# One transformer layer of a conformer on one core: another order of its head, of the LayerNorm sums and of one chunk, and other shares between engines

## The chip, the cores and the metric

The kernel runs on one core of one Trainium2 chip. The metric is the device time of one execution in microseconds. The median of three runs before the change is 1022.71 us (1021.47 to 1023.96).

The engines of the core are named as in the profile: PE is TensorE with its matmuls, PEld its weight loads, DVE is VectorE, ACT is ScalarE, POOL is GpSimd, and SP is SyncE, whose queue issues every DMA here.

## The reference, cut to what matters

With a depth of one, only the conformer layer on the 1024 latent tokens counts (the context is never read by it), followed by the MLP and a last norm. The width is 1024 and everything is float32.

```python
mod_l = (silu(c) @ w_mod + b_mod)                 # six vectors of 1024
sh1, s1, g1, sh2, s2, g2 = split(mod_l, 6)
h = rms_norm(x, norm1_g) * (1 + s1) + sh1
u = h @ w_pw1 + b_pw1                             # 1024 -> 2048
a, gate = split(u, 2)
u = a * sigmoid(gate)
u = dwconv(u, 31 taps, inside segments of 64 tokens) + b_dw
u = silu(layer_norm(u, ln_g, ln_b))
x = x + g1 * (u @ w_pw2 + b_pw2)
h = rms_norm(x, norm2_g) * (1 + s2) + sh2
x = x + g2 * (square(relu(h @ w1)) @ w2)          # 1024 -> 4096 -> 1024
return rms_norm(x, final_g)
```

## The kernel before

**Layout and blocks.** Tokens lie along the free axis and the 1024 channels in eight chunks of 128 partitions. The tokens are two blocks of 512, A (0) and B (1). Every product is done in three matmuls: a float32 operand is split into a rounded high part (a copy on ACT) and the remainder, the low part (a subtraction, L378, on DVE or POOL), and high x high, high x low and low x high are summed in a PSUM bank (L429 to L431, and L912 to L914 in the last product). One output unit of 128 channels for one block is eight times three matmuls of 128x512.

**The planner.** The program is written down as operations (class `Plan`, L86) with an engine, a modelled cost, buffers and a priority. `Plan.at` (L97) sets a base and every operation that follows gets the next rank above it. `Plan.run` (L125) simulates the engines: whenever one is free, it takes the ready operation of lowest rank whose tiles still find a place (`SLOTS`, `CAPS`, `KEEP`, L68 to L71). Operations that lie more than `NEAR` ranks past the oldest that is unplanned must leave some tiles free. The order so found is then emitted and is fixed: each engine takes its instructions in that order, whatever the real times are. A POOL operation planned after a DVE operation that is marked `port` is also made to wait for it (L231 to L235). The order of the DMAs on SP is found in the same way.

**The stages**, with their base ranks:

- *Head* (rank 0, L1045 to L1068). The eight chunks of x of block A are loaded, then the vector c, the identity and the small vectors. Squares on ACT and additions on DVE give one sum tile, which TensorE sums over partitions in turned form (four columns, L456). `rstd_of` (L498) takes the root on ACT, the reciprocal on DVE, spreads the four columns over a 128x512 tile (L519), and TensorE turns that into a row of factors in a bank (L528). Per chunk k, `mod_chunk` (L580) loads one 512 KB chunk of w_mod and reduces it against silu(c) (`csil`, L1054), for S1 and for SH1, on DVE (L587) or, elsewhere, on POOL with a second pass on ACT (L595, L600). `modulated` (L548) makes the split input, `first_weights` (L401) the split weights, and eight units of the first product are accumulated at once, k outermost. `warm` (L536) puts matmuls without use between, of 128 columns each.
- *Block B's input* (1010 to 1020), and then the rest of the first product: `PW1_ORDER` (1100 and up, L1100) lists pairs (block, chunk) of which each is two units (48 matmuls), a sigmoid on ACT and the gate on DVE (L640), through `first` (L1088).
- *Convolution* of block A (1200). Per chunk, 31 taps are shared out: on POOL (`POOL_TAPS`, ACT multiplies, POOL adds), on TensorE (`PE_TAPS`, a diagonal matrix per tap, L687, rank 1030), two or three as first taps on ACT, and the rest on DVE (L732). L742 and L751 join the partial sums.
- *LayerNorm* of block A (1300, `layer_norm`, L759): `cmean` holds the sum over channels of the convolution; TensorE sums what is left over partitions (`feed`, L448, L451). `direct` is how many chunks go to TensorE by themselves, while the others are added on another engine first. The mean is subtracted on DVE (L766), squares are summed the same way with `direct` = `LNA` or `LNB`, then root (L505), reciprocal (L507), multiplication (L780), silu and split.
- *Second convolution product* of block A (1400 and up, `pointwise2`), each output chunk with G1, S2 and SH2 through `mod_chunk`, on the engines of `G1_ENG`, `S2_ENG` and `SH2_ENG`. Then the second norm (1500), and the chunks of `PW1_LATE` (1600).
- *The MLP's first product* of block A, 32 units (2000 and up, `up_first`, L839), with block B's convolution, LayerNorm and second convolution product between them (`CONV_B`, `LN_B`, `PW2_B`).
- *The MLP's second product* (2200 and up, `mlp_joint`, L928), in eight groups that each combine two blocks and two halves into seven products instead of eight, each prepared by sums on DVE or POOL (`S_ENG`, `T_ENG`) and splits (`WLO_ENG`, `HLO_ENG`). The last group closes the final norms and stores the output.

Of the kernel before, what the change touches and what calls it, by code (L numbers as in the profile page):

```python
# [13 lines left out]
P = 128  # L14
D = 1024
# [23 lines left out]
POOL_TAPS = ((7, 8, 6, 9, 5, 5, 4, 3), (10, 9, 8, 7, 10, 6, 7, 5))  # L39

PW1_ORDER = (
    (0, 4), (0, 5), (1, 0), (1, 4), (1, 5),
    (0, 6), (0, 7), (1, 6), (1, 7), (1, 1),
)
PW1_LATE = ((1, 2), (1, 3))
# [3 lines left out]
PE_TAPS = ((2, 6, 2, 2, 2, 2, 5, 7), (0, 0, 2, 0, 0, 0, 0, 0))  # L49
PW2_LO, PW1_LO, WF_LO = "pool", "pool", ("dve",) * 8  # L50
UP_LO = ("dve", "pool")
S_ENG, T_ENG = ("pool", "pool", "dve", "dve"), ("dve", "dve", "dve", "dve")
GATE = 2
WLO_ENG, HLO_ENG = ("dve", "pool", "dve", "dve", "dve", "pool", "pool"), ("dve", "pool", "dve", "dve", "pool", "pool", "pool")
CM = (2, 1)
HEAD_DIRECT, LNA, LNB, N2B, FA = 0, 8, 2, 0, 0
TURNED = (True, False, False, False, False, False)
H1B_POOL = True
WARM = (8, 4, 6, 11)
# [3 lines left out]
S2_ENG, G1_ENG = ("pool", "pool", "dve", "pool", "pool", "pool", "pool", "pool"), ("pool", "pool", "pool", "dve", "dve", "pool", "dve", "pool")  # L63
SH2_ENG, G2_ENG = ("dve", "dve", "dve", "dve", "dve", "dve", "dve", "dve"), "dve"
# [5 lines left out]
NEAR = 120.0  # L70
CAPS = {"raw": 4, "head": 7, "w": 10, "tmp": 4, "tap": 3, "taps": 4, "acc": 8, "wave": 12}  # L71
# [10 lines left out]
class Op:  # L82
    __slots__ = ("eng", "costs", "emit", "prio", "turn", "table", "deps", "bufs", "left", "ready", "end", "after", "lag", "port")


class Plan:  # L86
# [38 lines left out]
    def run(self):  # L125
# [103 lines left out]
        for _, o in order:  # L229
            ins = o.emit()  # L230
# [15 lines left out]
def trunk(  # L246
# [50 lines left out]
    def c_dve(n):  # L297
        return 67 + 1.045 * n

    def c_stt(n):  # L300
        return 127 + 1.045 * n
# [138 lines left out]
    class Mean:  # L440
# [3 lines left out]
        def __init__(self, b, direct=1, eng="pool", turned=False):  # L444
            self.b, self.direct, self.eng, self.turned = b, direct, eng, turned
            self.n, self.sum, self.own, self.acc = 0, None, False, None

        def feed(self, x, first, last):  # L448
# [12 lines left out]
            if self.turned:  # L461
                plan.op("pe", 450 * QT, emit_turned, [x, ones], banks(self.acc))
            else:
                plan.op("pe", 1.67 * TB[self.b], emit, [x, ones], banks(self.acc))
# [33 lines left out]
    def rstd_of(mean, in_bank=True, hot=0):  # L498

        ((_, p),) = mean.acc  # L500
        if not mean.turned:
# [5 lines left out]
            plan.op("dve", 6.4 * TB[mean.b], lambda: dve.reciprocal(t(r), t(r)), [r], [r])  # L507
# [6 lines left out]
        warm(hot, root)  # L514
        plan.op("dve", 100, lambda: dve.reciprocal(root.t, root.t), [root], [root])
        spread = small(mean.b)
        plan.op(
# [8 lines left out]
        plan.op(  # L526
# [9 lines left out]
    def warm(n, after):  # L536
# [5 lines left out]
        def emit():  # L542
            for i in range(n):
                pe.matmul(t(p)[:, :P], ones.t, ones.t, start=True, stop=True)

        plan.op("pe", n * 220, emit, [ones, after], [p])
# [699 lines left out]
```

## Time and profile before

| | |
|---|---|
| median of 3 runs | 1022.71 us (1021.47 to 1023.96) |
| profiled execution, its own time | 1022.33 us |
| its span | 1020.5 us |
| PE busy | 980.4 us, 96% of the span, 4210 matmuls |
| DVE busy | 757.2 us, 74%, 1008 instructions |
| ACT busy | 520.1 us, 51%, 748 instructions |
| POOL busy | 513.8 us, 50%, 328 instructions |
| granted TensorE clock, mean | 0.981 |
| DMA | 125.28 MB, mean 123 GB/s |

A share of busy time is a mean over stages with different limits, so tables by stretch and timelines are read beside it. In a row of the timeline the first number is the start, the second the length, then engine, line, operation, tile written and tiles read, shapes and count; brackets give idle time of the engine before it and what ended it. A row that ends in a count merges neighbours of one line. A float32 matmul that isn't split, as in the sums (L451) and the taps (L687), appears as two instructions.

### The profile page before, as it was taken

The numbers are of one execution on the slowest core, as the hardware profiler recorded it, in microseconds if no ns is written. First come the engines' busy times: TensorE is split into PE (matmuls) and PEld (weight loads), VectorE is DVE, ScalarE is ACT, GpSimd is POOL, SyncE is SP. The second block draws the span as 40 slices with busy tenths as digits, with TensorE's granted clock in tenths as the row PEclk, the third lists the DMA queues.
The fourth block names the chain that finished last, engine by engine and source line by source line (L and its number), as shares of the span: only waits on it lengthen the run. The fifth ranks groups of instructions, "written<-read, shape, count | busy, mean of one in ns | idle before, by whom it ended". The sixth has DMA issues, their size and how long they took to land.

```text
span 1020.5 us, 11766 instructions
## 1 busy us (share of the span) xinstructions
PE 980.4 (96%) x4210; PEld 791.7 (78%) x4210; DVE 757.2 (74%) x1008; ACT 520.1 (51%) x748; POOL 513.8 (50%) x328
## 2 busy tenths in 40 slices
PE   5999999959999999999999999999999999999994
PEld 4878787638888888788888888888888888888882
DVE  5999999999699999863464473664747466494887
ACT  6488755185567765582473334342333434252443
POOL 0049999157744544322365536536363653634444
PEclk7999999979999999999999999999999999999998
DMA  9930025444426543644152413123141212303004
GB/s 358 404 114 1 1 83 208 163 164 165 145 83 215 182 158 116 224 157 155 67 192 87 141 41 104 62 83 124 62 144 42 99 66 83 125 1 124 1 1 165
DMA packets 52523, 125.28 MB, mean 123 GB/s; under 512 B 4464, under 2 KB 21104, under 8 KB 52464
## 3 DMA queue, kind: packets, MB, share of 16 engines
q1 hardware_dynamic: 52464, 124.53, 34.7%
q8 instruction: 33, 0.54, 0.2%
q14 instruction: 26, 0.21, 0.1%
HBM read 111.93 MB, written 12.58 MB: 122 GB/s over the span
## 4 chain that ended last, share of the span: by engine, by line
PE 75%; DVE 19%; POOL 2%; issue 2%; ACT 1%; DMA 1%; SPq 0%; POOLq 0%; DVEq 0%; ACTq 0%
PE bank L430 14%; PE bank L431 14%; PE bank L429 14%; DVE bank L732 12%; PE bank L913 10%; PE bank L914 10%; PE bank L912 10%; PE bank L451 2%; DVE big L378 1%; POOL small L378 1%; DVE bank L507 1%; DVE small L751 1%; POOL small L722 1%; DVE big L587 1%; DVE small L640 1%
## 5 line engine op out<-in xcount | busy, mean ns | idle before, releaser
L378 POOL TENSOR_TENSOR big<-big 128x1024 fp32r<-128x1024 f32 (+1 forms) x124 | 299.0, 2421 | 339.0 <-DVE big L378 155.6
L429 PE MATMUL bank<-big 128*128 128x512 f32 x896 | 355.0, 396 | 4.1 <-ACT big L371 3.9
L430 PE MATMUL bank<-big 128*128 128x512 f32 x896 | 350.0, 391 | 4.3 <-DVE big L378 3.2
L431 PE MATMUL bank<-big 128*128 128x512 f32 x896 | 349.7, 390 | 0.0
L800 DVE SCALAR_TENSOR_TENSOR small<-bank,mod,small 128x512 f32<-128x512 f32 x240 | 176.6, 748 | 197.1 <-PE bank L914 158.3
L378 DVE TENSOR_TENSOR big<-big 128x1024 fp32r<-128x1024 f32 (+2 forms) x160 | 198.6, 1262 | 27.4 <-POOL big L378 9.7
L872 ACT CAST big<-big 128x1024 fp32r<-128x1024 f32 x112 | 113.4, 1050 | 193.8 <-POOL big L378 60.0
L430 PEld LDWEIGHTS bank<-big 128*128 128x128 f32 x896 | 168.8, 188 | 42.8 <-DVE big L378 3.7
L732 DVE SCALAR_TENSOR_TENSOR bank<-small,vec,bank 128x464 f32<-128x464 f32 (+11 forms) x318 | 200.5, 697 | 1.7
L429 PEld LDWEIGHTS bank<-big 128*128 128x128 f32 x896 | 168.9, 188 | 41.8 <-ACT big L371 4.1
L431 PEld LDWEIGHTS bank<-big 128*128 128x128 f32 x896 | 168.8, 188 | 35.2
L912 PE MATMUL bank<-big 128*128 128x512 f32 x448 | 174.7, 390 | 0.0
L913 PE MATMUL bank<-big 128*128 128x512 f32 x448 | 174.3, 389 | 0.0
L914 PE MATMUL bank<-big 128*128 128x512 f32 x448 | 174.3, 389 | 0.0
L722 POOL TENSOR_TENSOR small<-small 128x400 f32<-128x400 f32 (+4 forms) x109 | 113.3, 1067 | 50.4 <-DVE big L378 27.8
L391 ACT CAST big<-big 128x1024 fp32r<-128x1024 f32 x92 | 95.6, 1043 | 23.4 <-POOL big L378 11.0
L912 PEld LDWEIGHTS bank<-big 128*128 128x128 f32 x448 | 84.1, 188 | 17.7 <-issue 0.2
L913 PEld LDWEIGHTS bank<-big 128*128 128x128 f32 x448 | 84.1, 188 | 17.6 <-issue 0.2
L914 PEld LDWEIGHTS bank<-big 128*128 128x128 f32 x448 | 84.1, 188 | 17.4
L378 POOL TENSOR_TENSOR small<-small 128x512 f32<-128x512 f32 x39 | 52.1, 1340 | 83.3 <-DVE big L378 44.3
L493 ACT ACTIVATE small<-small 128x512 f32<-128x512 f32 x64 | 39.0, 628 | 64.2 <-DVE small L800 60.0
L717 ACT ACTIVATE small<-small,vec 128x400 f32<-128x400 f32 (+4 forms) x109 | 62.9, 629 | 0.0
(68 smaller groups left out, 597.6 us busy)
## 6 DMA issues: line engine op xcount, KB each, us to landing
big<-in_w SPq DMA_DIRECT2D x96, 512.0 KB, 3.9
big<-in_wmod SPq DMA_DIRECT2D x48, 512.0 KB, 5.4
big<-in_wpw SPq DMA_DIRECT2D x28, 512.0 KB, 5.3
hidden<-small SPq DMA_DIRECT2D x32, 256.0 KB, 2.4
big<-hidden SPq DMA_DIRECT2D x16, 512.0 KB, 3.9
small<-in_xA SPq DMA_DIRECT2D x16, 256.0 KB, 5.2
big<-in_wfirst SPq DMA_DIRECT2D x8, 512.0 KB, 10.2
small<-in_xB SPq DMA_DIRECT2D x16, 256.0 KB, 6.1
```

What stands on the lines that cost most here:

```text
L378: lambda: eng_of[o.eng].tensor_tensor(out=out(), in0=a(), in1=b(), op=op), r, w, part=part, port=port,
L391: plan.op("act", c_act(D), lambda: act.copy(t(wh), t(raw)), [raw], [wh], also=[wl])
L429: pe.matmul(o, wh, hi(a)[:, s], start=first, stop=False)
L430: pe.matmul(o, wh, lo(a)[:, s], start=False, stop=False)
L431: pe.matmul(o, wl, hi(a)[:, s], start=False, stop=last)
L722: return pool.tensor_tensor(out=dst, in0=dst, in1=seg(t(m))[:, :, tt], op=ALU.add)
L732: dve.scalar_tensor_tensor(out=dst, in0=src, scalar=w, in1=dst, op0=ALU.mult, op1=ALU.add)
L800: lambda s=s, p=p: dve.scalar_tensor_tensor(out=t(x)[:, s], in0=cut(s, p), scalar=scale.t, in1=t(x)[:, s], op0=ALU.mult, op1=ALU.add,),
L872: plan.op("act", c_act(D), lambda: act.copy(t(h), t(x)), [x], [h], also=[l])
L912: pe.matmul(t(p), t(wh)[:, cs], t(hh)[:, ns], start=first and k == 0, stop=False, skip_group_check=not first)
L913: pe.matmul(t(p), t(wh)[:, cs], t(hl)[:, ns], start=False, stop=False, skip_group_check=not first)
L914: pe.matmul(t(p), t(wl)[:, cs], t(hh)[:, ns], start=False, stop=k == 1, skip_group_check=not first)
```

## The change

**Head.** The load of c and its silu move ahead of x and of the squares, so that the roots' table is loaded only once on ACT. The reductions of S1 (all but the first) and of SH1 are held until the spread tile (L519) is written (`hold`). `first_weights` moves behind `modulated`. The warm-up matmuls have other counts and are placed behind the fifth square, the turned sum and the spread product; a warm-up is now tied to an operation and no longer to a buffer.

**LayerNorm.** The sums of block A's mean and of its squares on TensorE (`feed`) get rank 1030, ahead of the first products (1100 and up). `rstd_of` places warm-ups behind the last sum and behind the reciprocal of block A's LayerNorm. `CM` gives block A's mean one direct chunk instead of two, and `LNB` block B's squares none instead of two.

**Order.** Chunk (1,2) moves from `PW1_LATE` to the end of `PW1_ORDER`; from the eleventh entry on, the loads of weights wait for the gate of the entry three places earlier (`PW1_BACK`). (0,6) and (0,7) come ahead of (1,4) and (1,5). Block B's taps on TensorE get rank 1399 instead of 1030.

**Shares.** Taps on POOL: block A 47 to 45, block B 62 to 56. Taps on TensorE: A 28 to 25, B 2 to 8. Reductions of G1, S2 and SH2 on DVE: 3, 1 and 8 before, 0, 2 and 1 after; the others are on POOL. Some sums and splits of the last product change engines.

**Planner.** `NEAR` is 250 instead of 120, one more tile for POOL's taps is allowed, and DVE's operations are modelled as 8 ns and 23 ns longer.

```diff
-POOL_TAPS = ((7, 8, 6, 9, 5, 5, 4, 3), (10, 9, 8, 7, 10, 6, 7, 5))
+POOL_TAPS = ((7, 7, 6, 9, 4, 5, 4, 3), (10, 9, 8, 4, 5, 7, 8, 5))
...
-    (0, 4), (0, 5), (1, 0), (1, 4), (1, 5),
-    (0, 6), (0, 7), (1, 6), (1, 7), (1, 1),
+    (0, 4), (0, 5), (1, 0), (0, 6), (0, 7),
+    (1, 4), (1, 5), (1, 6), (1, 7), (1, 1), (1, 2),
...
-PW1_LATE = ((1, 2), (1, 3))
+PW1_LATE = ((1, 3),)
+TAP_PRIO = (1030, 1399)
+PW1_BACK = 3
...
-PE_TAPS = ((2, 6, 2, 2, 2, 2, 5, 7), (0, 0, 2, 0, 0, 0, 0, 0))
+PE_TAPS = ((2, 6, 2, 3, 2, 2, 2, 6), (0, 0, 2, 3, 3, 0, 0, 0))
...
-S_ENG, T_ENG = ("pool", "pool", "dve", "dve"), ("dve", "dve", "dve", "dve")
+S_ENG, T_ENG = ("pool", "dve", "dve", "dve"), ("dve", "pool", "dve", "dve")
...
-WLO_ENG, HLO_ENG = ("dve", "pool", "dve", "dve", "dve", "pool", "pool"), ("dve", "pool", "dve", "dve", "pool", "pool", "pool")
-CM = (2, 1)
-HEAD_DIRECT, LNA, LNB, N2B, FA = 0, 8, 2, 0, 0
+WLO_ENG, HLO_ENG = ("dve", "pool", "pool", "dve", "dve", "dve", "dve"), ("dve", "pool", "pool", "dve", "pool", "dve", "pool")
+CM = (1, 1)
+HEAD_DIRECT, LNA, LNB, N2B, FA = 0, 8, 0, 0, 0
...
-WARM = (8, 4, 6, 11)
+WARM = (6, 6, 7, 11)
...
-S2_ENG, G1_ENG = ("pool", "pool", "dve", "pool", "pool", "pool", "pool", "pool"), ("pool", "pool", "pool", "dve", "dve", "pool", "dve", "pool")
-SH2_ENG, G2_ENG = ("dve", "dve", "dve", "dve", "dve", "dve", "dve", "dve"), "dve"
+S2_ENG, G1_ENG = ("pool", "pool", "dve", "pool", "pool", "pool", "dve", "pool"), ("pool", "pool", "pool", "pool", "pool", "pool", "pool", "pool")
+SH2_ENG, G2_ENG = ("pool", "pool", "pool", "pool", "pool", "pool", "dve", "pool"), "dve"
...
-NEAR = 120.0
-CAPS = {"raw": 4, "head": 7, "w": 10, "tmp": 4, "tap": 3, "taps": 4, "acc": 8, "wave": 12}
+NEAR = 250.0
+CAPS = {"raw": 4, "head": 7, "w": 10, "tmp": 4, "tap": 4, "taps": 4, "acc": 8, "wave": 12}
...
-        return 67 + 1.045 * n
+        return 75 + 1.045 * n
...
-        return 127 + 1.045 * n
+        return 150 + 1.045 * n
...
-                plan.op("pe", 1.67 * TB[self.b], emit, [x, ones], banks(self.acc))
+                o = self.fed = plan.op("pe", 1.67 * TB[self.b], emit, [x, ones], banks(self.acc))
+                if self.prio:
+                    o.prio = self.prio
...
-            plan.op("dve", 6.4 * TB[mean.b], lambda: dve.reciprocal(t(r), t(r)), [r], [r])
+            warm(hot, p.writers[-1] if p is not r else mean.fed)
+            o = plan.op("dve", 6.4 * TB[mean.b], lambda: dve.reciprocal(t(r), t(r)), [r], [r])
+            warm(hot, o)
...
-        warm(hot, root)
...
-    cmean = [Mean(0, CM[0]), Mean(1, CM[1])]
+    cmean = [Mean(0, CM[0], prio=1030), Mean(1, CM[1])]
...
-                plan.op("pe", 1.67 * reach(s, k), emit, [diag, u], [p]).prio = 1030
+                plan.op("pe", 1.67 * reach(s, k), emit, [diag, u], [p]).prio = TAP_PRIO[b]
...
-        ms = Mean(b, direct, turned=TURNED[1 + 2 * b])
+        ms = Mean(b, direct, turned=TURNED[1 + 2 * b], prio=1030 if b == 0 else None)
...
-        rstd = rstd_of(ms)
-        if b == 0:
-            warm(WARM[3], rstd)
+        rstd = rstd_of(ms, True, WARM[3] if b == 0 else 0)
...
-    xs0 = load_x(0)
     craw = new("big", [P, D], F32, "raw")
     plan.op("dma", 1460, lambda: sp.dma_start(t(craw), cvec.partition_broadcast(P)), w=[craw], lag=2000)
+    xs0 = load_x(0)
     load(ident, eye, P)
     load(vec, vecs, NVEC)
+    plan.op("act", c_act(D), lambda: act.activation(csil.t, t(craw), AF.Silu), [craw], [csil], "silu")
     ms = Mean(0, HEAD_DIRECT, "dve", TURNED[0])
-    warm(WARM[0], xs0[3])
     for k in range(KC):
         sq = add_square(ms, xs0[k])
-    plan.op("act", c_act(D), lambda: act.activation(csil.t, t(craw), AF.Silu), [craw], [csil], "silu")
+        if k == 4:
+            warm(WARM[0], sq.writers[-1])
     preload(AF.Sqrt, "sqrt", sq)
-    r0, r0_bank = rstd_of(ms, False, WARM[1])
-    warm(WARM[2], r0)
+    warm(WARM[1], ms.fed)
+    r0, r0_bank = rstd_of(ms, False)
+    warm(WARM[2], ms.spread_fed)
...
-        mod_chunk(S1, k, cap="head")
-        mod_chunk(SH1, k, "dve", "head")
-        wf.append(first_weights(k, WF_LO[k]))
+        mod_chunk(S1, k, cap="head", hold=[ms.spread] if k else ())
+        mod_chunk(SH1, k, "dve", "head", hold=[ms.spread])
         scale_column(sc1[k], mod[S1][k], C_N1, k)
         h1[0].append(modulated(0, xs0[k], r0 if k else r0_bank, sc1[k], mod[SH1][k], True))
+        wf.append(first_weights(k, WF_LO[k]))
...
-                w_of[c, h] = weights(wpw1[2 * c + h], PW1_LO, (), h1[0][KC - 1 :])
+                w_of[c, h] = weights(wpw1[2 * c + h], PW1_LO, after, h1[0][KC - 1 :])
...
-        first(*bc)
+        first(*bc, [us[PW1_ORDER[n - PW1_BACK]]] if n >= 10 else ())
```

More of the change, by code (lines that the diff above doesn't have):

```diff
@@ L82 @@
 class Op:
-    __slots__ = ("eng", "costs", "emit", "prio", "turn", "table", "deps", "bufs", "left", "ready", "end", "after", "lag", "port")
+    __slots__ = ("eng", "costs", "emit", "prio", "turn", "table", "deps", "bufs", "left", "ready", "end", "after", "lag", "port", "ins")
 class Plan:
@@ L229, in run @@
         for _, o in order:
-            ins = o.emit()
+            ins = o.ins = o.emit()
             if o.eng == "dve" and o.port:
@@ L440, in trunk, with __init__ @@
     class Mean:
-        def __init__(self, b, direct=1, eng="pool", turned=False):
+        def __init__(self, b, direct=1, eng="pool", turned=False, prio=None):
+            self.prio = prio
             self.b, self.direct, self.eng, self.turned = b, direct, eng, turned
@@ L461, in feed @@
             if self.turned:
-                plan.op("pe", 450 * QT, emit_turned, [x, ones], banks(self.acc))
+                self.fed = plan.op("pe", 450 * QT, emit_turned, [x, ones], banks(self.acc))
             else:
-                plan.op("pe", 1.67 * TB[self.b], emit, [x, ones], banks(self.acc))
+                o = self.fed = plan.op("pe", 1.67 * TB[self.b], emit, [x, ones], banks(self.acc))
+                if self.prio:
+                    o.prio = self.prio
         def add(self, x):
@@ L513, in rstd_of @@
         )
-        warm(hot, root)
         plan.op("dve", 100, lambda: dve.reciprocal(root.t, root.t), [root], [root])
         spread = small(mean.b)
-        plan.op(
+        mean.spread = plan.op(
             "dve", c_stt(TB[mean.b]),
@@ L525, in rstd_of @@
         )
-        plan.op(
+        mean.spread_fed = plan.op(
             "pe", 1.67 * TB[mean.b],
@@ L543, in emit @@
             for i in range(n):
-                pe.matmul(t(p)[:, :P], ones.t, ones.t, start=True, stop=True)
-        plan.op("pe", n * 220, emit, [ones, after], [p])
+                ins = pe.matmul(t(p)[:, :P], ones.t, ones.t, start=True, stop=True)
+                if i == 0 and after.eng != "pe":
+                    behind(ins, after.ins)
+        plan.op("pe", n * 213, emit, [ones], [p], gate=[after])
     def modulated(b, x, rstd, scale, shift, in_place, eng="dve"):
@@ L578, in modulated, with mod_chunk @@
         return out
-    def mod_chunk(v, i, eng="dve", cap="raw", gate=()):
+    def mod_chunk(v, i, eng="dve", cap="raw", gate=(), hold=()):
         raw = new("big", [P, D], F32, cap)
@@ L589, in mod_chunk @@
                 ),
-                [raw, csil, vec], [raw, m], port=True,
+                [raw, csil, vec], [raw, m], port=True, gate=hold,
             )
@@ L1086, in trunk, with first @@
     w_of = {}
-    def first(b, c):
+    def first(b, c, after=()):
         out = []
```

## The prediction, made before the changed kernel was run

> **What bounds the kernel now.** I read the page's head first, then busy time by stretch, then the timeline of the one long stretch in which TensorE has nothing to do. First the span and a table of stretches (start:end, length, then busy us and instructions of PE, PEld, DVE, ACT, POOL, then the granted clock, DMA share, GB/s).
>
> ```profile
> span 1020.5 us, 11766 instructions
> 10.00:23.60 13.60, 8.39 (x32) 6.60 (x32) 9.17 (x17) 10.39 (x17) 0.00 (x0) 0.57 1.03 406
> 23.60:66.00 42.40, 42.40 (x187) 35.12 (x188) 40.98 (x70) 22.00 (x35) 2.01 (x1) 1.00 0.85 330
> 150.00:199.80 49.80, 49.69 (x203) 37.49 (x202) 48.74 (x80) 21.74 (x43) 30.04 (x23) 1.00 0.53 185
> 199.80:228.20 28.40, 14.96 (x45) 7.40 (x44) 27.48 (x47) 19.82 (x32) 14.98 (x8) 0.79 0.46 157
> 228.20:290.00 61.80, 61.77 (x258) 50.25 (x259) 49.32 (x73) 37.58 (x60) 43.13 (x31) 0.96 0.44 154
> 350.00:410.00 60.00, 60.00 (x267) 49.67 (x266) 59.50 (x91) 39.04 (x61) 26.89 (x25) 1.00 0.39 136
> 540.00:1002.90 462.90, 462.90 (x2041) 382.88 (x2040) 289.30 (x328) 178.59 (x212) 232.33 (x99) 1.00 0.22 77
> 1002.90:1020.50 17.60, 3.68 (x8) 1.06 (x7) 11.89 (x14) 3.68 (x6) 7.46 (x6) 0.74 0.64 238
> ```
>
> TensorE is full before and after the hole from 199.8 to 228.2, and there it sets the pace: 462.9 us over 2041 matmuls is 0.227 us each, so an output unit of 24 matmuls takes 5.44 us, and one chunk of the first product for one block (two units) 10.9 us. What can be won lies in the head (23.6 us), in the hole, in TensorE work that goes away, and in the tail (17.6 us), whose order the change hardly touches. The profiled execution took 1022.33 us, 1.83 more than its span; I sum against it, and the median of the runs shown, 1022.71, is 0.4 above. About 0.2% (2 us) is what a measurement can tell from no change.
>
> The hole in the timeline (start, length, engine, line; the last three rows are from the chain that ended last):
>
> ```profile
> 196.66 0.69 DVE L751 TENSOR_TENSOR small<-bank,small 128x512 f32<-128x512 f32 x1
> 199.62 2.74 PE L451 MATMUL bank<-small,ones 128*128 128x512 f32 x6
> 207.12 4.87 DVE L766 TENSOR_TENSOR small<-small,bank 128x512 f32<-128x512 f32 x8
> 208.66 9.15 PE L451 MATMUL bank<-small,ones 128*128 128x512 f32 x16 [6.30 <-ACT small L493]
> 217.65 2.62 PE L544 MATMUL bank<-ones 128*128 128x128 f32 x22
> 218.55 3.37 DVE L507 RECIPROCAL bank<-bank 128x512 f32<-128x512 f32 x1 [0.85 <-ACT bank L505]
> 221.95 4.87 DVE L780 TENSOR_TENSOR small<-small,bank 128x512 f32<-128x512 f32 x8
> 228.23 0.79 PE L430 MATMUL bank<-big 128*128 128x512 f32 x1 [3.24 <-DVE big L378]
> 229.45 0.43 PE bank L429
> 234.03 0.23 PE bank L429
> 501.16 0.86 PE bank L451 x2
> ```
>
> Block A's convolution ends with L751 at 197.4. Its mean is summed on TensorE (three 512-wide sums of two instructions) by 202.4, but VectorE subtracts it only from 207.1, because other work stands ahead in its written order. Squares, eight sums, root, reciprocal, multiply, silu and split follow; dense products return at 228.2, at half pace (0.43 us) until about 233. The old row of products simply ran out.
>
> **The change part by part.** *The hole.* Chunk (1,2) of the first product, 10.9 us of TensorE, moves from behind block A's second norm to the end of that row. Its cost stays; it now lies where TensorE was idle. The LayerNorm sums (1030) rank above products (1100 and up), so they wait for at most the group of three in flight (0.68 us). Ten sums remain (mean 3 to 2, squares 8), at 0.86 us each at full clock (the last row above): 8.6 us.
>
> When is the chain done? Three rows: VectorE's taps, its modulation reductions, and TensorE's taps alone in a stretch of the table.
>
> ```profile
> L732 DVE SCALAR_TENSOR_TENSOR bank<-small,vec,bank 128x456 f32<-128x456 f32 (+10 forms) x158 | 101.6, 698 | 1.7
> L587 DVE CUSTOM_DVE_ANT_0 big<-big,csil,vec x36: 1273/1280/3490, 14.7 to 348.4; 128x1024 f32<-128x1024 f32 x36
> 150.00:199.80 49.80, 9.78 (x24) 4.20 (x24) 1.00 0.53 185
> ```
>
> A VectorE tap is 101.6/158 = 0.64 us. Block A has 157 of them now and 162 after (POOL 47 to 45, TensorE 28 to 25), +3.2; one reduction of 1.28 that stands among them goes to POOL: the convolution ends at 199.3. Mean by 201.0, eight subtractions (4.9) to 205.9, last square and sum to 208, root 0.7, reciprocal 3.4, multiplies from 212.1; products were dense 6.3 us after the multiplies began (228.2 less 221.95), so at 218.4. TensorE's own side: a tap there is two instructions, 9.78/12 = 0.82 us; three fewer end the old row at 196.9 instead of 199.4, and 10.9 and 8.6 more end at 216.4. On paper 2 us stay idle. The order is fixed ahead, and VectorE came 4.7 us late to its subtraction; I add half of that and take 4 us, with 0 and 12 as ends. The old stretch cost 28.4 us and another 2.3 at half pace (12 matmuls in 5.06 us instead of 2.7). The new one has 8.6 + 4 of it: **-18.1**.
>
> [...]
>
> *TensorE work.* Its taps go from 30 to 33 (A 28 to 25, B 2 to 8): +3 x 0.82 = **+2.5**. Block B's rank below the first products and need chunks that come late, so they lie in full stretches. Block B's LayerNorm sums go from three to one: **-1.7**; two more additions on POOL lie under 24-matmul units. Warm-up matmuls stay in idle time; if that is gone, 22 of them cost 2.6 us (the L544 row).
>
> *The head.*
>
> ```profile
> 12.13 1.87 PE L456 MATMUL bank<-ones,small 128*128 128x1 f32 x8 [7.37 <-DVE small L378]
> 10.76 1.28 ACT L1031 ACT_TABLE_LOAD   x1
> 12.37 1.28 ACT L1054 ACT_TABLE_LOAD   x1
> 13.66 1.06 ACT L1054 ACTIVATE csil<-big 128x1024 f32<-128x1024 f32 x1
> 14.73 1.28 ACT L512 ACT_TABLE_LOAD   x1
> 17.16 0.17 DVE L515 RECIPROCAL root<-root 128x4 f32<-128x4 f32 x1
> 20.91 0.75 DVE L553 SCALAR_TENSOR_TENSOR small<-small,sc,bank 128x512 f32<-128x512 f32 x1 [1.52 <-ACT small L533]
> ```
>
> Sums are done at 14.0, but the root starts only behind the last of three table loads, at 16.0, and its reciprocal at 17.2, behind two reductions. With cvec's load and silu first, one root load is left, before the sums end; holding the reductions for the spread removes the second wait. That is 17.16 - 14.4 = 2.8 us. Against it: cvec's 512 KB ahead of x delay the squares by up to 1.3 us at 406 GB/s; and VectorE, 40.98 of 42.4 us busy from 23.6 to 66, must deliver just as much sooner. I take **-2.2**, ends 0 and -3.
>
> *Shares and what comes later.* Nine more reductions move from VectorE to POOL (G1, S2, SH2), and each needs a pass on ACT (1.06 us for this width).
>
> ```profile
> L595 POOL TENSOR_TENSOR big<-big,csil x12: 2342/2378/2427, 99.4 to 266.7; 128x1024 f32<-128x1024 f32 x12
> L378 POOL TENSOR_TENSOR big<-big 128x1024 fp32r<-128x1024 f32 x2 | 4.7, 2350 | 25.1 <-DVE mod L587 18.1 <-ACT big L391 6.9
> 258.75 2.67 DVE L587 CUSTOM_DVE_ANT_0 big<-big,csil,vec 128x1024 f32<-128x1024 f32 x1
> L800 DVE SCALAR_TENSOR_TENSOR small<-bank,mod,small 128x512 f32<-128x512 f32 x8 | 6.0, 750 | 11.0 <-PE bank L431 11.0
> 409.75 1.41 DVE L751 TENSOR_TENSOR small<-bank,small 128x512 f32<-128x512 f32 x2
> 464.54 0.75 DVE L800 SCALAR_TENSOR_TENSOR small<-bank,mod,small 128x512 f32<-128x512 f32 x1 [4.24 <-PE bank L431]
> 497.18 0.75 DVE L800 SCALAR_TENSOR_TENSOR small<-bank,mod,small 128x512 f32<-128x512 f32 x1 [3.56 <-PE bank L431]
> 509.29 2.07 DVE L572 SCALAR_TENSOR_TENSOR big<-small,mod,big 128x512 fp32r<-128x512 f32 x3
> 500.57 0.60 ACT L843 ACTIVATE small<-bank 128x512 f32<-128x512 f32 x1 [1.03 <-POOL small L378]
> 517.94 0.59 ACT L843 ACTIVATE small<-bank 128x512 f32<-128x512 f32 x1
> ```
>
> POOL gets 9 x 2.38 = 21.4 us. From 150 to 228.2 it has 19.8 + 13.4 = 33.2 idle, much of it behind VectorE's reductions (18.1 in one wait). ACT has 28 + 8.6 idle there for about 10. So I cost it at nothing for TensorE; if the cover is gone, block A's weight splits on POOL come late (second rival). VectorE gains 11.5 us, and chunk (1,2) gives it taps in the 11.0 us in which it waited for TensorE, against 2 more taps of block B (1.3).
>
> TensorE reaches the time around 450 some 20 us ahead of before. Block B's convolution, which ends at 411 and then holds up block B's second product (464), must gain nearly as much. It gets 2.2 from the head, 9.8 from the earlier restart, 11.5 and part of 11.0: 23 or more. Besides, four units of the up product (21.8 us; ACT's L843 rows from 500 to 518) are still there to bridge block B's norm. So no new hole is priced. From 540 on each engine but TensorE has over a third of its time free (289 of 463 for VectorE); one 1.2 us operation more on VectorE per group, one of 2.4 fewer on POOL, and the planner's farther look ahead (250) cost nothing, ends -1 and +4.
>
> **Sum**: 1022.33 - 18.1 + 2.5 - 1.7 - 2.2 = 1002.8, say **1003**, 1.9% faster.
>
> **The rivals.**
> 1. *A wait takes the place of the hole.* TensorE's order is fixed. A sum ranked ahead of products and ready later than planned stops chunk (1,2) behind it. For: VectorE's 4.7 us delay. Against: the cost of a tap is raised to what the rows show. Price: idle 12 instead of 4, and 1.3 for the head: 1012.
> 2. *Slower: POOL's queue holds the split of (1,2)'s weights.* These splits are on POOL, behind nine more multiplications, and POOL waits for VectorE by order. If the 25.1 us of such waits in the L378 POOL row stay and fall ahead of the split, TensorE stands there, and the LayerNorm sums behind it. 1003 + 25.1 = 1028; it decides from 20 us of delay. Against: reductions on VectorE, which caused 18.1 of it, go, and the weights are gated two chunks ahead (some 22 us).
> 3. *Port.* The L587 at 258.75 took 2.67 instead of 1.28 beside a POOL operation. If each of nine POOL multiplications stops VectorE for its 2.38, block B's convolution loses 21.4 of its 23, and the bridge of 21.8 less about 13 for block B's norm (last L800 of its second product, 497.9, to its first three splits, 511) leaves 9: hole 20 - 2 - 9 = 9 us, 1012. [...]
> 4. *Nothing*: the hole only moves to block B's norm, 1022: VectorE's convolution would have to gain nothing.
>
> **How the numbers follow.** Forecast 0.60 (own range 998 to 1009), first rival 0.14, third 0.10, nothing 0.05, slower 0.11. Faster 0.84, same 0.05, slower 0.11. Leaving out the slower case and small remainders, the range goes from 995 (1003 less 0.8 for the head, 4 for a full hole and 1 later is 997, and 2 for a measurement) to 1019, between the 1012 of two rivals and the 1022 and 1028 left out in part.
>
> **What would show it.** Right: chunk (1,2)'s matmuls between 195 and 220, L766 within 1 us of the mean sum, a full clock there, dense products of block A's second convolution product near 216, one table load between the squares and the first root, products from about 21.4, no gap from 220 to 1000. Wrong: TensorE waiting over 5 us for ACT squares or a POOL split near 200; POOL full from 200 to 290; a TensorE gap between 400 and 520; VectorE's reductions in the head delaying the eighth input chunk.

## The result, and the profile after

| | before | after |
|---|---|---|
| median | 1022.49 us (1021.47 to 1023.96, 4 runs) | 1010.25 us (1009.33 to 1010.97, 4 runs) |
| ratio, 95% interval | | 0.9883 [0.9869, 0.9897] |
| profiled execution, its own time | 1022.33 us | 1009.33 us |
| first dense products | 23.58 us | 22.22 us |
| block A's convolution ends | 197.35 us | 199.93 us |
| dense products behind the LayerNorm | 228.2 us | 222.88 us |
| last product ends | 1002.88 us | 988.60 us |

The change makes the kernel 12.2 us faster. The forecast was 1003 (995 to 1019): the direction and the range held, and a third of the gain is missing. The medians are compared with runs of before on the same chip, the traces with the profiled execution of before. All the single edits below are planned anew by the planner, so the orders differ in more than the edit; the waits of each trace, more than its time alone, carry the conclusions. Three executions of two of these edits, of 1110, 1719 and 2580 us, lie far from the others of their kernels and are left out of the figures.

The head of the page of after, busy time by engine (span 1007.5 us):

```profile
PE 977.7 (97%) x4234; PEld 791.7 (79%) x4234; DVE 770.4 (76%) x1005; ACT 525.3 (52%) x767; POOL 510.6 (51%) x324
```

Busy time by stretch of after (columns as in the prediction's table), cut at the same events as there:

```profile
150.00:198.95 48.95, 48.95 (x203) 37.74 (x201) 47.11 (x77) 30.01 (x57) 48.57 (x33) 1.00 0.65 239
198.95:222.90 23.95, 21.39 (x100) 15.30 (x100) 23.88 (x41) 22.08 (x35) 15.48 (x9) 1.00 0.45 150
222.90:290.00 67.10, 66.10 (x282) 52.72 (x283) 65.57 (x92) 48.05 (x80) 49.52 (x35) 1.00 0.43 149
...
410.00:540.00 130.00, 129.85 (x569) 106.51 (x568) 71.48 (x73) 71.94 (x96) 45.27 (x30) 1.00 0.41 144
540.00:988.60 448.60, 448.55 (x1975) 370.12 (x1973) 302.39 (x330) 173.99 (x207) 210.10 (x90) 1.00 0.23 76
988.60:1007.50 18.90, 3.70 (x9) 1.44 (x8) 10.60 (x12) 2.71 (x5) 7.96 (x7) 0.72 0.59 222
```

The LayerNorm's stretch now has 21.4 of 24 us busy at a granted clock of 1.00, against 15 of 28.4 at 0.79; warm-ups, which do no useful work, are 4.8 of the 21.4 and 2.6 of the 15. From there to the last product TensorE lacks about 1 us before 290 and nearly nothing later. The tail got longer: 18.9 us against 17.6.

TensorE (L454 sums, L550 warm-ups, L431 and L432 products), DVE and ACT in the timeline of that stretch of after:

```profile
199.25 0.68 DVE L759 TENSOR_TENSOR small<-bank,small 128x512 f32<-128x512 f32 x1
199.98 1.12 PE L454 MATMUL bank<-small,ones 128*128 128x512 f32 x2 [1.03 <-DVE small L759]
201.25 4.86 DVE L774 TENSOR_TENSOR small<-small,bank 128x512 f32<-128x512 f32 x8
203.02 2.74 PE L454 MATMUL bank<-small,ones 128*128 128x512 f32 x6
206.29 4.45 PE L454 MATMUL bank<-small,ones 128*128 128x512 f32 x10
207.75 0.63 ACT L498 ACTIVATE small<-small 128x512 f32<-128x512 f32 x1
210.56 1.28 ACT L510 ACT_TABLE_LOAD   x1
212.56 3.36 DVE L513 RECIPROCAL bank<-bank 128x512 f32<-128x512 f32 x1
215.46 1.28 ACT L639 ACT_TABLE_LOAD   x1
215.95 3.08 DVE L786 TENSOR_TENSOR small<-small,bank 128x512 f32<-128x512 f32 x5
216.04 5.07 PE L550 MATMUL bank<-ones 128*128 128x128 f32 x44
217.46 1.28 ACT L791 ACT_TABLE_LOAD   x1
220.87 0.48 PE L431 MATMUL bank<-big 128*128 128x512 f32 x1
222.88 0.50 PE L432 MATMUL bank<-big 128*128 128x512 f32 x1 [1.53 <-DVE big L380]
```

The mean's subtraction (L774) starts 0.15 us behind the mean's sum; the old 4.7 us of delay are gone. Useful TensorE work ends at 216.04. From there warm-ups fill 4.8 us and another 2.0 pass around a single product, until the low part of the first split (L380) is there. With the 1.03 us ahead of the mean's sum that is 7.9 us without useful work.

### The profile page after: what moved, and what is told of

It is laid out like the page before. It is cut to its first block, busy times and chain, and to the rows that moved or that the text cites. A ratio compares the mean times of both kernels' runs of the same rounds, so it can differ in the third digit from the quotient of the medians.

```text
span 1007.5 us, 11799 instructions
## 1 busy us (share of the span) xinstructions
PE 977.7 (97%) x4234; PEld 791.7 (79%) x4234; DVE 770.4 (76%) x1005; ACT 525.3 (52%) x767; POOL 510.6 (51%) x324
## 4 chain that ended last, share of the span: by engine, by line
PE 82%; DVE 11%; issue 2%; ACT 2%; POOL 1%; DMA 1%; SPq 0%; POOLq 0%; DVEq 0%
PE bank L432 17%; PE bank L431 17%; PE bank L433 17%; PE bank L919 9%; PE bank L920 9%; PE bank L918 9%; DVE bank L740 2%; DVE big L380 2%; PE bank L695 2%; DVE big L595 2%; POOL small L380 1%; DVE small L380 1%; DVE bank L513 1%; DVE small L774 1%; DMA small<-in_xA 1%
## 5 line engine op out<-in xcount | busy, mean ns | idle before, releaser
L380 POOL TENSOR_TENSOR big<-big 128x1024 fp32r<-128x1024 f32 (+1 forms) x116 | 278.0, 2410 | 332.5 <-DVE big L380 108.7
L431 PE MATMUL bank<-big 128*128 128x512 f32 x896 | 355.9, 397 | 0.9 <-ACT small L639 0.9
L432 PE MATMUL bank<-big 128*128 128x512 f32 x896 | 348.9, 389 | 1.8 <-DVE big L380 1.5
L806 DVE SCALAR_TENSOR_TENSOR small<-bank,mod,small 128x512 f32<-128x512 f32 x240 | 177.6, 748 | 156.2 <-PE bank L920 126.5
L380 DVE TENSOR_TENSOR big<-big 128x1024 fp32r<-128x1024 f32 (+2 forms) x168 | 218.3, 1327 | 36.6 <-ACT big L878 9.3
L740 DVE SCALAR_TENSOR_TENSOR bank<-small,vec,bank 128x424 f32<-128x424 f32 (+10 forms) x325 | 202.8, 695 | 2.2 <-ACT bank L677 1.0
L432 PEld LDWEIGHTS bank<-big 128*128 128x128 f32 x896 | 168.2, 188 | 40.4 <-issue 3.7
L431 PEld LDWEIGHTS bank<-big 128*128 128x128 f32 x896 | 168.2, 188 | 39.4 <-issue 3.8
L730 POOL TENSOR_TENSOR small<-small 128x392 f32<-128x392 f32 (+4 forms) x101 | 106.1, 1075 | 39.2 <-ACT small L725 15.5
L380 POOL TENSOR_TENSOR small<-small 128x512 f32<-128x512 f32 x42 | 56.8, 1357 | 92.4 <-DVE big L380 48.4
L918 PEld LDWEIGHTS bank<-big 128*128 128x128 f32 x448 | 84.1, 188 | 17.7 <-issue 0.2
L725 ACT ACTIVATE small<-small,vec 128x392 f32<-128x392 f32 (+4 forms) x101 | 57.7, 628 | 0.0
```

The costliest lines, as they stand in the source:

```text
L380: lambda: eng_of[o.eng].tensor_tensor(out=out(), in0=a(), in1=b(), op=op), r, w, part=part, port=port,
L431: pe.matmul(o, wh, hi(a)[:, s], start=first, stop=False)
L432: pe.matmul(o, wh, lo(a)[:, s], start=False, stop=False)
L730: return pool.tensor_tensor(out=dst, in0=dst, in1=seg(t(m))[:, :, tt], op=ALU.add)
L740: dve.scalar_tensor_tensor(out=dst, in0=src, scalar=w, in1=dst, op0=ALU.mult, op1=ALU.add)
L806: lambda s=s, p=p: dve.scalar_tensor_tensor(out=t(x)[:, s], in0=cut(s, p), scalar=scale.t, in1=t(x)[:, s], op0=ALU.mult, op1=ALU.add,),
```

## The experiments

**The chunk back.** The change with (1,2) behind block A's second norm again.

```diff
-    (1, 4), (1, 5), (1, 6), (1, 7), (1, 1), (1, 2),
+    (1, 4), (1, 5), (1, 6), (1, 7), (1, 1),
-PW1_LATE = ((1, 3),)
+PW1_LATE = ((1, 2), (1, 3))
```

> The changed kernel with chunk (1,2) moved back behind the second norm, all else kept. Theory (the chunk fills the hole, and its 10.9 us of TensorE are what the hole was short of): TensorE's idle and warm-up time around block A's LayerNorm grows from 7.9 us by about 10, and the time from 1010.3 to 1019 to 1021 us. Rival (the rank of the sums and the shares carry the gain, the chunk is only shifted): within 3 us of 1010.

Measured: 1022.38 us (1017.67 to 1023.25, 10 runs), ratio to before 0.9994 [0.9979, 1.0009]. The stretches around its LayerNorm:

```profile
195.60:220.40 24.80, 17.70 (x64) 10.80 (x63) 24.00 (x40) 22.05 (x39) 20.14 (x11) 0.79 0.46 157
220.40:232.00 11.60, 9.25 (x36) 7.29 (x35) 10.96 (x20) 11.31 (x20) 5.04 (x8) 0.85 0.24 77
```

The hole is back, and the clock falls to 0.79 in it. The gain needs the chunk that fills it: without it all the other edits together come out even with before, a little slower than the 1019 to 1021 expected. It needs more than the chunk, as the next edits show.

**The sums without their rank.** Both `prio` arguments of the LayerNorm sums taken away.

```diff
-    cmean = [Mean(0, CM[0], prio=1030), Mean(1, CM[1])]
+    cmean = [Mean(0, CM[0]), Mean(1, CM[1])]
-        ms = Mean(b, direct, turned=TURNED[1 + 2 * b], prio=1030 if b == 0 else None)
+        ms = Mean(b, direct, turned=TURNED[1 + 2 * b], prio=None)
```

> The changed kernel with the sums of block A's mean and squares back at their own rank, behind the first products; chunk (1,2) stays where the change put it. Theory (chunk and rank need each other): the mean's sum waits for the 10.9 us of chunk (1,2), the chain of the LayerNorm ends 6 to 9 us later and the hole returns behind the chunk: 1016 to 1019 us. Rival (the products end when the convolution ends, so rank changes nothing): 1009 to 1012 us.

Measured: 1016.78 us (1016.07 to 1017.75, 4 runs), ratio 0.9948 [0.9932, 0.9964], 6.5 us slower than the change. Timeline:

```profile
205.22 1.88 PE L454 MATMUL bank<-small,ones 128*128 128x512 f32 x4
208.66 4.86 DVE L774 TENSOR_TENSOR small<-small,bank 128x512 f32<-128x512 f32 x8
210.05 6.28 PE L454 MATMUL bank<-small,ones 128*128 128x512 f32 x14 [2.95 <-ACT small L498]
219.29 2.07 PE L454 MATMUL bank<-small,ones 128*128 128x512 f32 x2 [2.96 <-ACT small L498]
```

TensorE does all products first, up to 205.2; only then the mean is summed, and the subtraction starts 7.4 us later than in the change. The chunk covers little, since the chain that it should cover starts behind it: a hole of 26.0 us (205.2 to 231.2) follows. Still the kernel is 5.6 us faster than the one without the chunk.

**The chunk alone on the kernel before**, with the loads of weights held three entries back, as in the change; and then with the sums' rank too.

```diff
-    (0, 6), (0, 7), (1, 6), (1, 7), (1, 1),
+    (0, 6), (0, 7), (1, 6), (1, 7), (1, 1), (1, 2),
-PW1_LATE = ((1, 2), (1, 3))
+PW1_LATE = ((1, 3),)
...
-        first(*bc)
+        first(*bc, [us[PW1_ORDER[n - 3]]] if n >= 10 else ())
```

> The kernel before with one part of the change: chunk (1,2) at the end of the first products, its weights' loads held as in the change. Theory: without the rank the sums come behind the chunk, so the hole only moves by some 10 us and the gain is small: 1016 to 1022 us. Rival (the chunk alone fills the hole): 1010 to 1013 us.

```diff
-    cmean = [Mean(0, CM[0]), Mean(1, CM[1])]
+    cmean = [Mean(0, CM[0], prio=1030), Mean(1, CM[1])]
-        ms = Mean(b, direct, turned=TURNED[1 + 2 * b])
+        ms = Mean(b, direct, turned=TURNED[1 + 2 * b], prio=1030 if b == 0 else None)
```

> The kernel before with two parts of the change: chunk (1,2) at the end of the first products, and the sums of block A's LayerNorm ranked above the first products. Theory: the two together carry most of the change, 1009 to 1013 us. Rival (the shares between engines and the head are needed for it): 1016 us or more.

Measured: the chunk alone 1023.94 us (1022.81 to 1024.52, 10 runs), ratio 1.0017 [1.0007, 1.0026]: a hole of 28 us from 209.3 to 237.5 in place of the one of 28.4 from 199.8. With the rank 1029.97 us (1028.93 to 1030.49, 4 runs), ratio 1.0075 [1.0060, 1.0091]. There TensorE is full from 200 to 245, as hoped, and then stands. Besides, it idles 5.0 us from 150 to 200, most of it where the sums that now rank ahead wait for L754 (3.2) and for POOL (1.1). Timeline of the second kernel:

```profile
245.44 12.24 DVE L735 SCALAR_TENSOR_TENSOR bank<-small,vec,bank 128x488 f32<-128x488 f32 x20
257.58 0.68 DVE L754 TENSOR_TENSOR small<-bank,small 128x512 f32<-128x512 f32 x1
258.32 0.80 PE L429 MATMUL bank<-big 128*128 128x512 f32 x1 [12.89 <-DVE small L754]
```

The product at 258.32 waits for L754. It needs no result of that line; L754 is the last reader of a bank in which VectorE has summed block B's taps (L735, 20 of them ahead of it), so the product waits for the bank. A hole of one kind became a wait of another, 12.9 us long, and the clock fell in it (granted clock 0.60 from 245 to 259). The expectation that chunk and rank would bring nearly the whole gain fell.

**The cost model added, or the shares added.** Both on the kernel with chunk and rank: DVE's operations modelled as in the change, or the nine reductions moved to POOL.

```diff
-        return 67 + 1.045 * n
+        return 75 + 1.045 * n
-        return 127 + 1.045 * n
+        return 150 + 1.045 * n
```

> The kernel before with chunk (1,2), the rank of the sums, and the change's longer modelled times of VectorE. Theory (the 12.9 us stall at 245, where TensorE waits for a bank that block B's taps hold, comes from an order planned with too short VectorE taps): the stall goes or shrinks below 5 us, 1014 to 1020 us. Rival (it comes from the shares, so the model alone doesn't matter): 1027 to 1032 us.

```diff
-S2_ENG, G1_ENG = ("pool", "pool", "dve", "pool", "pool", "pool", "pool", "pool"), ("pool", "pool", "pool", "dve", "dve", "pool", "dve", "pool")
-SH2_ENG, G2_ENG = ("dve", "dve", "dve", "dve", "dve", "dve", "dve", "dve"), "dve"
+S2_ENG, G1_ENG = ("pool", "pool", "dve", "pool", "pool", "pool", "dve", "pool"), ("pool", "pool", "pool", "pool", "pool", "pool", "pool", "pool")
+SH2_ENG, G2_ENG = ("pool", "pool", "pool", "pool", "pool", "pool", "dve", "pool"), "dve"
```

> The kernel before with chunk (1,2), the rank of the sums, and nine reductions of G1, S2 and SH2 moved from VectorE to POOL. Theory (VectorE's reductions are what pushes its work past TensorE's need after the hole): the stall at 245 goes, 1012 to 1018 us. Rival (the modelled times decide): 1026 to 1032 us.

Measured: with the model 1034.91 us (1034.50 to 1035.92, 4 runs), ratio 1.0119 [1.0104, 1.0134]; the same wait for the same line is 17.7 us there, so the model alone doesn't cure it, and the time lies above both ranges. With the shares 1021.54 us (1020.04 to 1022.78, 9 runs), ratio 0.9987 [0.9978, 0.9997], 8.4 us less than without them. TensorE's waits in that trace (line, what it waited for, sum, times, longest):

```profile
PE bank L452 <- POOL small L378: 4.0, 2, 2.9
PE bank L452 <- DVE small L754: 3.7, 3, 2.6
```

The 12.9 us are gone: taking nine reductions of 1.28 us off VectorE, 11.5 us in all, brings block B's taps in time. The sums (L452) wait 7.7 us, over half of it where they stand ahead of products in the order (4.4 us of idle from 150 to 200); that idle time isn't new, it was 5.0 without the shares. The stall went as expected; the time stayed 3.5 us above the 1012 to 1018 expected. So chunk, rank and shares together are only even with before. The 11 us from there to the change lie in what is left of it (modelled times, head, order, taps, planner), which was not added to them part by part.

**The reductions back.** The same lines put back in the change.

> The changed kernel with the reductions of G1, S2 and SH2 on the engines of before (twelve instead of three on VectorE). Theory of the shares: VectorE loses 11.5 us again, part of it in or just behind the hole, and a wait on VectorE comes back: 1015 to 1022 us. Rival (VectorE has the time, and the ACT passes of POOL's reductions, two of which stood among the squares, cost more): 1006 to 1011 us.

Measured: 1026.82 us (1024.96 to 1029.12, 5 runs), ratio 1.0036 [1.0022, 1.0049], 16.6 us slower than the change. The trace is of the execution of 2580 us, 2.5 times as long as the others at a granted clock of 1.00, so its waits tell nothing of the 16.6 us. Where they went stays open, though the pair above shows one place. I had expected at most 1022.

**The cost model back** in the change (67 and 127 again).

> The changed kernel planned with the shorter VectorE times of before. Theory of the model: sums ranked ahead stand in TensorE's order earlier than their squares are ready, and waits of 3 to 10 us appear: 1013 to 1020 us. Rival (the shares and the chunk carry it): 1009 to 1012 us.

Measured: 1022.44 us (1018.50 to 1023.66, 10 runs), ratio 0.9994 [0.9983, 1.0005], above both ranges. The trace is of the fastest run, whose head is 3.0 us shorter than that of the change (last section). Timeline:

```profile
209.33 0.69 DVE L759 TENSOR_TENSOR small<-bank,small 128x512 f32<-128x512 f32 x1
210.17 1.82 PE L454 MATMUL bank<-small,ones 128*128 128x512 f32 x2 [3.18 <-DVE small L759]
```

Not the sums stand too early, as I had thought: block A's convolution itself ends at 210.0 instead of 199.9, behind the chunk's products, and a hole of 27 us (206.8 to 233.7) follows. Why the shorter modelled cost places the last taps 10 us later was not tried by itself.

**Both late chunks** in the old row's place.

```diff
-    (1, 4), (1, 5), (1, 6), (1, 7), (1, 1), (1, 2),
+    (1, 4), (1, 5), (1, 6), (1, 7), (1, 1), (1, 2), (1, 3),
-PW1_LATE = ((1, 3),)
+PW1_LATE = ()
```

> The changed kernel with chunk (1,3) moved as well, so that 10.9 us more of first products lie behind (1,1). Theory (the hole still lacks about 7.9 us of work: 4.8 of warm-up and 3 of idleness): TensorE is full through the LayerNorm and the time falls by 4 to 8 us, 1002 to 1006 us. Rival (the gain comes back as a wait elsewhere, as the stall of 12.9 us did in the kernel before with chunk and rank: VectorE or banks): 1009 to 1020 us.

Measured: 1025.45 us (1024.71 to 1027.73, 5 runs), ratio 1.0036 [1.0023, 1.0049]. That is above both ranges. Timeline at the two norms:

```profile
222.44 1.90 DVE L380 TENSOR_TENSOR big<-small,big 128x512 fp32r<-128x512 f32 x3
...
226.34 5.07 PE L550 MATMUL bank<-ones 128*128 128x128 f32 x44
...
293.26 0.80 PE L431 MATMUL bank<-big 128*128 128x512 f32 x1 [8.00 <-ACT big L576]
```

At the first norm 5.9 of the 7.9 us stay: 1.0 ahead of the mean's sum, and 4.8 of warm-ups. The useful row now ends at 226.3, and three low parts of the next products' input are written by 224.3 (L380), so TensorE would have had useful work; but its written order has the 44 warm-ups first, and here they only delay. And block A's second norm, which (1,3) bridges in the change, lies open: 13.1 us from 280.1. Each norm needs a chunk of its own: two for the first leave none for the second.

**The gate of (1,2) late**, so that ACT doesn't change tables between root and silu.

```diff
+GATE_LATE = ((1, 2),)
...
-                [p, vec], [sig], "sigmoid", part=True,
+                [p, vec], [sig], "sigmoid", part=True, gate=hold,
...
+    for bc in late_gates:
+        gate(*bc, hold=list(vA[3].writers))
```

> The changed kernel with the sigmoid and gate of chunk (1,2) held until the fourth input of block A's second convolution product is split, so that ACT loads the silu table right behind the root. Theory (two table loads and a sigmoid between root and silu, 215.5 to 218.7, delay the first split by about 2 us, and TensorE idles then): dense products 2 us sooner after the multiplies begin, 1007.5 to 1009 us. Rival (the splits on VectorE, behind eight multiplies and other work, end last, or the two banks that wait for the gate are missed): 1009.5 to 1015 us.

Measured: 1012.07 us (1011.61 to 1013.90, 4 runs), ratio 0.9902 [0.9888, 0.9915]. The silu's table is loaded at 213.58 there, and the multiplies run unbroken. The head of this trace is 3.0 us shorter than that of the change (last section). Stretches:

```profile
213.00:218.60 5.60, 5.42 (x46) 5.00 (x45) 5.60 (x11) 5.47 (x9) 5.60 (x4) 1.00 0.01 1
218.60:221.80 3.20, 0.50 (x2) 0.20 (x2) 3.20 (x6) 3.14 (x6) 1.75 (x1) 0.84 0.00 0
221.80:225.00 3.20, 3.20 (x8) 2.52 (x9) 3.20 (x6) 3.14 (x6) 0.00 (x0) 0.50 0.69 232
```

From the first multiply (212.97) to dense products (221.78) it takes 8.8 us instead of 6.9, since the low part of the split comes on VectorE behind all eight multiplies and five taps (3.25 us), as the rival said. And 3.2 us with a single product bring the half clock back: 8 matmuls in 3.2 us. What ACT gained, VectorE's new order took back; what the two table loads at 215.46 and 217.46 of the change cost by themselves stays open.

**A longer warm-up in the head**: 28 instructions behind the second square instead of 12 behind the fifth.

```diff
-WARM = (6, 6, 7, 11)
+WARM = (14, 6, 7, 11)
...
-        if k == 4:
+        if k == 1:
```

> The changed kernel with the first warm-up behind the second square instead of the fifth and 14 instead of 6 matmuls, so that TensorE is busy from about 7 us to the turned sum. Theory (one profile had the turned sum in 1.05 and the spread product in 1.10 us, with products from 19.2, the others 1.87 and 1.4 to 2.0, from 21.4 to 22.2; what differs is only whether the clock had risen): turned sum 1.1 us, products from 19 to 20, 1007 to 1008.5 us. Rival (the clock is low at 13 us whatever stands before, or VectorE's reductions decide the start): products from 21.4 or later, 1009.5 to 1011 us.

Measured: 1014.31 us (1013.90 to 1015.25, 5 runs), ratio 0.9922 [0.9908, 0.9935]. Timeline:

```profile
7.76 4.97 PE L550 MATMUL bank<-ones 128*128 128x128 f32 x28 [7.76 <-ACT small L498]
13.28 1.05 PE L459 MATMUL bank<-ones,small 128*128 128x1 f32 x8 [0.54 <-DVE small L380]
...
19.68 0.50 PE L432 MATMUL bank<-big 128*128 128x512 f32 x1 [0.29 <-DVE big L580]
...
223.75 0.79 PE L432 MATMUL bank<-big 128*128 128x512 f32 x1 [3.61 <-DVE big L380]
224.34 0.63 PE L433 MATMUL bank<-big 128*128 128x512 f32 x1
```

The head is 2.5 us shorter, as expected. But block A's convolution ends only 0.9 us earlier (198.99); a new order makes the low part 3.6 us late at 223.75 (four taps stand ahead of it on VectorE), half pace follows, and the last product ends at 993.3, 4.7 us later than in the change. What the head won was not passed on.

**The shares of the last product back.** Only groups of the MLP's second product differ; up to it the order is that of the change.

```diff
-S_ENG, T_ENG = ("pool", "dve", "dve", "dve"), ("dve", "pool", "dve", "dve")
+S_ENG, T_ENG = ("pool", "pool", "dve", "dve"), ("dve", "dve", "dve", "dve")
-WLO_ENG, HLO_ENG = ("dve", "pool", "pool", "dve", "dve", "dve", "dve"), ("dve", "pool", "pool", "dve", "pool", "dve", "pool")
+WLO_ENG, HLO_ENG = ("dve", "pool", "dve", "dve", "dve", "pool", "pool"), ("dve", "pool", "dve", "dve", "pool", "pool", "pool")
```

> The changed kernel with the sums and splits of the MLP's second product on the engines of before; the order up to there stays as in the change. Theory (the tail grew from 17.7 to 18.9 us because block A's last reciprocal stands on VectorE ahead of four instead of three additions of block B, with the new shares): TensorE full from 540 on as before, the last product within 0.5 us of 988.6 after the start, a tail of 17.6 to 17.9 us, 1008.5 to 1009.7 us. Rival (the new shares keep TensorE fed and the old ones would not, at this kernel's pace): gaps between 540 and 990 and 1011 us or more.

Measured: 1007.71 us (1005.88 to 1010.08, 5 runs), ratio 0.9854 [0.9840, 0.9867]: the best median of all. Its profiled execution is its slowest run (1010.08): the last product ends at 989.93, 1.3 us later than in the change (TensorE waits 1.3 us for DVE's L806), and the tail takes 18.4 us, where 17.6 to 17.9 were expected. That trace can't tell where the median's 2.5 us come from. Two of its five runs took 1005.9, and the others 1.8 to 4.2 us more; the head's clock (2 to 3 us, last section) may be part of that, but those runs have no trace. So this version is at least as good as the change; that the shares of the last product are the reason is not shown.

## Why the prediction was right, and where it was short

By its own sum, against the profiled execution (1022.33 to 1009.33; forecast 1002.8, so 6.5 us short):

| step | forecast | measured |
|---|---|---|
| hole of block A's LayerNorm | -18.1 | about -14.2 |
| head | -2.2 | -1.4 |
| taps and block B's sums on TensorE | +0.8 | taken as costed |
| tail | 0 | +1.3 |
| rest, by subtraction | 0 | +0.5 (TensorE waits 0.9 us for a sigmoid until 284.1) |

*The hole, right in mechanism, 3.9 us mis-sized.* The term was 8.6 us of sums and 4 of idle time; the sums came as costed (20 instructions, two of them already at 189), the idle time was 7.9. TensorE's side was right: its useful work ends at 216.04, forecast 216.4. The chain was nearly on time up to the subtractions: convolution 199.9 (199.3), mean 201.1 (201.0), subtractions 206.1 (205.9). Then the last sum ends at 210.7 instead of 208. Eight sums of 0.86 us take 6.9 us on TensorE whatever the squares do; the first starts at 203.02, and the written order puts three products behind the third. The last square (207.75 to 208.38) is ready before its sum's turn comes, so it is TensorE's own row that ends the step, where the prediction had let one sum follow the last square. After that the root's table is loaded only behind other passes that ACT has from 208.28 to 210.54 (210.56 to 211.84), 1.1 us beyond the sums. So the multiplies start at 215.95 instead of 212.1, and dense products come 6.9 us later instead of 6.3, as a gate and a tap stand ahead of the low part on VectorE. I had taken the chain as a sum of durations with VectorE's delay alone; the row of sums on TensorE and ACT's order were the missing part. Of the 4 us, half of VectorE's old delay was an allowance, and that delay did not come (0.15 us): that it covered part of the rest is luck. The two ends for this term (0 and 12) did hold it. (The sum has dense products at 218.4, the list of signs near 216; they came at 222.9.)

*No half pace.* The full clock came as forecast: it is 1.00 from 198.95 to 290, where before had 0.79 in the hole and 0.96 behind it. That the old 2.3 us at half pace would go with the hole was my estimate. In the change the warm-ups leave a stretch of 2.0 us with one product, and the next products run at full pace (14 in 3.1 us); with 3.2 us (late gate) and 4.1 us (longer warm-up in the head) they run at half, 14 matmuls at 0.43 us, some 2.8 us lost. The length of a gap doesn't decide alone: in the kernel without the sums' rank a wait of 2.95 us leaves the full pace (14 instructions in 6.28 us), and one of 2.96 us brings half (two in 2.07). In the records of the granted clock the spells at half in these kernels and in the one before, between the head and the tail, last 3.41 us or two or three times that: 6.83 from 205.94 and 10.24 from 223.00 (before), 6.83 from 220.80 (late gate) and from 222.74 (longer warm-up), 3.41 from 219.28 (without rank). By these gaps I estimate that the 44 warm-ups of the change, without which 6.8 us would lie open there (4.8 and 2.0), pay for themselves, while in the kernel with both chunks they delay products; a kernel without them was not tried.

*The head, 0.8 us short.* TensorE, ACT and VectorE in the timeline of the head of after:

```profile
11.42 1.28 ACT L1037 ACT_TABLE_LOAD   x1
13.02 1.86 PE L459 MATMUL bank<-ones,small 128*128 128x1 f32 x8 [0.70 <-DVE small L380]
14.74 2.91 PE L550 MATMUL bank<-ones 128*128 128x128 f32 x12
14.92 0.26 ACT L519 ACTIVATE root<-bank,eps 128x4 f32<-128x4 f32 x1 [1.03 <-PE bank L459]
15.43 0.69 DVE L525 SCALAR_TENSOR_TENSOR small<-ident,root 128x512 f32<-128x512 f32 x1
17.44 1.92 PE L534 MATMUL bank<-small,ones 128*128 128x512 f32 x2
```

One table load is left between squares and root, and the root follows its sum at once (16.03 to 14.92), as forecast. But the turned sum starts 0.9 us later than before (12.13 to 13.02): the squares stand behind c's load and its silu (to 6.42) on ACT. That costs less than the 1.3 that the prediction had as the bound, and more than the 0.6 that it took. A second loss the prediction didn't see: the spread tile (L525) is written at 16.12, but its product starts at 17.44, behind twelve warm-up instructions, which take 2.91 us at half pace (1.58 in the two quick heads of the last section). So of the 1.9 us by which the reciprocal starts sooner (17.16 to 15.21), 0.8 are left at the spread product (18.21 to 17.44) and 1.4 at the first dense products. The prediction had said that warm-ups stay in idle time.

*The tail, costed at nothing, +1.3 us.* VectorE, TensorE and POOL at the end of after:

```profile
982.49 3.37 DVE L513 RECIPROCAL bank<-bank 128x512 f32<-128x512 f32 x1
985.77 2.65 DVE L806 SCALAR_TENSOR_TENSOR small<-bank,mod,small 128x512 f32<-128x512 f32 x4
...
990.51 3.70 PE L454 MATMUL bank<-small,ones 128*128 128x512 f32 x8 [1.91 <-POOL small L380]
994.95 3.37 DVE L513 RECIPROCAL bank<-bank 128x512 f32<-128x512 f32 x1 [2.59 <-ACT bank L510]
```

Block A's reciprocal stands ahead of four additions of block B, POOL gets the squares' sums late, and TensorE's last sums wait for it until 990.51. Block B's reciprocal starts 6.35 us behind the last product; before, 5.08 (1007.96 less 1002.88). The change didn't touch this order by name; the planner found another one. "Hardly touches" was not a reason to price it at nothing. With the shares of the last product back, TensorE waits 0.3 us for POOL there instead of 1.9, and block B's reciprocal starts 5.50 us behind the last product; so they are part of it.

*The shares, right as costed, for half a reason.* I had expected no cost for TensorE and a gain for block B's convolution that keeps the hole from moving to block B's norm near 450. No gap came there, and block B's mean is subtracted at 402.9 instead of 415.6. But the pair with chunk and rank shows that VectorE's lateness without the shares stops TensorE much earlier, at 245, through a bank that block B's taps hold. I had priced engines and queues, but no bank.

*The rivals.* The first (a sum ranked ahead and ready late) had the right place with a small price, 1.03 us; in the kernels of before with chunk and rank such waits made most of 4.4 to 5.0 us of idle time. The second, slower by POOL's queue, and the third, the port, fell: no wait of TensorE for a weight split near 200, and no gap from 410 to 540. The fourth (the hole only moves) was wrong for the change. For the chunk alone a hole did only move, but within block A's norm, not to block B's as that rival had it.

## What to carry to other kernels

Work that is moved into a hole helps only if the chain that it covers is started ahead of it, and if the other engines keep up with the earlier restart: added to the kernel before, the chunk without rank gained nothing, chunk with rank lost 8 us, and only the shares paid that back, to even. Price a moved step in every resource that joins two streams, the banks too, and follow the chain through the written order of each engine on it, not only the slowest one. Where an order is planned as a whole, a small edit anywhere changes all of it, so a trace's named wait tells more than the time of a single edit.

## What the runs showed of the hardware that was not expected

Behind the same warm-up in the head, TensorE's clock rises early in only two of seven traces. Timeline of the kernel with the cost model back, whose head has the change's code:

```profile
9.15 2.93 PE L550 MATMUL bank<-ones 128*128 128x128 f32 x12 [9.15 <-ACT small L498]
12.67 1.05 PE L459 MATMUL bank<-ones,small 128*128 128x1 f32 x8 [0.58 <-DVE small L380]
15.23 1.10 PE L534 MATMUL bank<-small,ones 128*128 128x512 f32 x2
...
19.20 0.50 PE L432 MATMUL bank<-big 128*128 128x512 f32 x1 [0.28 <-DVE big L580]
```

Its turned sum takes 1.05 us where after's takes 1.86, the spread 1.10 instead of 1.92, and products are dense at 19.20 instead of 22.22. The same holds for the kernel with the late gate (1.05, 19.27). In the records of the granted clock, full speed begins at 12.44 and 12.59 us in these two. In the five other traces of this head (the change among them) it begins between 17.83 and 20.75, the turned sum takes 1.86 or 1.87, and products are dense from 21.4 to 22.2. (Tables by stretch show 1.00 for the head of the change all the same, as no record stands ahead of the first rise.) The first warm-up takes 2.93 us in the change and in both quick heads, and starts at 9.21 in a slow head (without rank) and at 9.22 in a quick one (late gate). Full speed begins 3.3 to 3.4 us after the start of the first warm-up in the two quick heads and 8.3 to 11.4 us after it in the five slow ones. So 2 to 3 us of the start differ between traces without a cause that they show; that two executions of one kernel can differ by that much for it alone is an estimate from them. With 4.97 us of warm-up, in one trace, full speed began at 11.11, 3.35 us after its start, and the turned sum took 1.05.
